# Stick-breaking attention: two subtractions per score tile written for VectorE instead of GpSimd

## The chip, the cores and the metric

The kernel runs on one core of a Trainium2 chip. Its time is the device time of one execution in microseconds (us). The core has five engines that work side by side and wait for each other through semaphores: TensorE (PE in the rows; its weight loads are PEld), VectorE (DVE), ScalarE (ACT), GpSimd (POOL) and SyncE (SP), which issues DMAs here. Each engine works through its own instructions in a fixed order.

## The reference

The reference is a block of two mixers, a memory attention and a mixture of experts on 1024 rows of width 1024, all in float32. Only one part of the first mixer matters here, the stick-breaking attention, 4 heads of width 64:

```python
for i in range(t // SB_BLOCK):                      # 8 blocks of 128 queries
    n_keys = (i + 1) * SB_BLOCK
    z = einsum('bhtd,bhsd->bhts', q_blk, k_blk) * scale
    strict = s_pos < t_pos
    log_beta = log_sigmoid(z)
    log_1m_beta = where(strict, log_sigmoid(-z), 0.0)
    between = cumsum(log_1m_beta, axis=3, reverse=True) - log_1m_beta
    weights = where(strict, exp(log_beta + between), 0.0)
    outs.append(einsum('bhts,bhsv->bhtv', weights, v_blk))
```

The weight of a key is the exponential of its logit less the sum of log(1 + exp(z)) over that key and all later ones. The kernel makes log(1 + exp(z)) as log(1 + exp(min(z, 40))) plus the part of z that lies over 40.

## The kernel before

The first mixer runs twice, once for each half of the rows (`first_mixer(h, ...)`, h = 0 and 1). In each half it makes projections (`proj_fm`, `proj_tm`), whose weights come in slabs: ScalarE rounds a slab to `whi`, VectorE subtracts to get `wlo`, and TensorE multiplies three times (`mm3`, lines 140 to 142, tile `mm`). Two further mixers of gated linear attention (`gla_pair`, tiles `qp`, `kp`, `d`, `E`, `cmp`, `at`) run in the same stretch.

The stick-breaking attention goes over 4 query blocks per half, 2 pairs of heads, chunks of at most 512 keys and the 2 heads of a pair. One pass through the innermost loop is called a unit here: 16 units in the first half, 32 in the second; 24 of the 48 are 512 keys wide, and 8 each are 128, 256 and 384 wide. A unit is a chain over four engines:

1. TensorE makes the logits (line 761), ScalarE copies them to `z`, and on the block's diagonal GpSimd masks 128 columns (line 768).
2. VectorE writes `e` = min(z, 40) (tile `ze`), GpSimd writes `cu` = z - e.
3. ScalarE overwrites `e` with exp(e) and then with ln(1 + e).
4. VectorE's running sum (line 775) adds `e` and `cu` from the last key to the first; where more chunks follow, its end is copied to `cy`.
5. GpSimd writes z = z - cu, ScalarE takes exp(z) in place.
6. TensorE transposes the result (tile `tp`), VectorE copies it to `pt` (line 787), TensorE multiplies with the values (tile `os`, line 790).

The tiles `z`, `ze`, `zc` (for `cu`) and `zp` (for `pt`) have two buffers each, so two units are under way at a time. Their instructions, the projections and the gated attention are merged into one order per engine by a scheduler when the program is built; units come first in it where they are ready, and the projections' matmuls fill what is left of TensorE. The scheduler has its own idea of how long an instruction takes. The helpers `TT` (line 41, two tensors) and `TS` (line 45 with one operation, line 47 with two) record most of VectorE's and GpSimd's instructions, so a line alone does not say which instruction it is; the tile names do.

Of the kernel before, what the change touches and what calls it, by code (L numbers as in the profile page):

```python
# [27 lines left out]
def block_kernel(  # L28
# [6 lines left out]
    pe, act, dve, pool, sp = nc.tensor, nc.scalar, nc.vector, nc.gpsimd, nc.sync  # L35

    def A(o, i, f, **kw):
        act.activation(out=o, in_=i, func=f, **kw)  # L38

    def TT(o, a, b, op, eng=None):  # L40
        (eng or dve).tensor_tensor(out=o, in0=a, in1=b, op=op)  # L41

    def TS(o, a, s1, op0, s2=None, op1=None, eng=None):
        if op1 is None:
            (eng or dve).tensor_scalar(out=o, in0=a, scalar1=s1, scalar2=None, op0=op0)
        else:
            (eng or dve).tensor_scalar(out=o, in0=a, scalar1=s1, scalar2=s2, op0=op0, op1=op1)

    def STT(o, a, s, b, op0, op1, **kw):
        dve.scalar_tensor_tensor(out=o, in0=a, scalar=s, in1=b, op0=op0, op1=op1, **kw)  # L50

    MUL, ADD, SUB, MAX, MIN, POW = (
        ALU.mult, ALU.add, ALU.subtract, ALU.max, ALU.min, ALU.pow)
# [10 lines left out]
    def bank(tag, bufs):  # L64
        return ps[0].tile([128, 512], F32, name=tag, tag=tag, bufs=bufs)
# [4 lines left out]
    def tpb():  # L70
        return bank("tp", 2)
# [121 lines left out]
    def transpose4(o, srcs):  # L193

        for j, s in enumerate(srcs):
            pe.transpose(o[0:s.shape[-1], j * 128:j * 128 + s.shape[0]], s, ident[0:s.shape[0], 0:s.shape[0]])  # L196
# [232 lines left out]
    with ad_stack:  # L429
# [15 lines left out]
        for k in range(8):  # L445
            gk = 8 // G
            j = k % gk
            if j == 0:
# [12 lines left out]
                for i in range(8):  # L461
                    w = was[k // gk * 8 + i][:, 1]
# [12 lines left out]
               eng=pool if k < 6 else dve)  # L475
# [217 lines left out]
    def first_mixer(h, hT, ahead):  # L693
# [36 lines left out]
        for pr in range(2):  # L730
            g = tpb()
            pe.matmul(out=g, lhsT=w2[:, 128 * pr:128 * pr + 128], rhs=lrs, start=True, stop=True)
            e = a1.tile([128, HALF], F32, name="spe", tag="E", bufs=3)
# [13 lines left out]
        for t in range(4):  # L747

            with tc.high_priority(offset=0):
                n = 4 * h + t  # L750
                os_ = bank("os", 1)
                carry0 = [True]
                for pr in range(2):
                    carry = [None, None]
                    for s0 in range((n // 4) * 4, -1, -4):
                        ns = min(4, n + 1 - s0)
                        w = ns * 128
                        for hh in range(2):
                            r = slice(64 * hh, 64 * hh + 64)
                            zp = bank("z", 1)  # L760
                            pe.matmul(out=zp[:, 0:w], lhsT=qc[r, pr, t * 128:(t + 1) * 128],
                                      rhs=kc_full[r, pr, s0 * 128:s0 * 128 + w], start=True, stop=True)
                            z = a1.tile([128, HALF], F32, name="z", tag="z", bufs=2)
                            e = a1.tile([128, HALF], F32, name="ze", tag="ze", bufs=2)
                            A(z[:, 0:w], zp[:, 0:w], AF.Copy)
                            if s0 + ns - 1 == n:
                                dg = slice(w - 128, w)
                                pool.affine_select(out=z[:, dg], in_=z[:, dg], pattern=[[-1, 128]], compare_op=ALU.is_gt,
                                                   fill=-30000.0, base=0, channel_multiplier=1)
                            TS(e[:, 0:w], z[:, 0:w], 40.0, MIN)  # L770
                            cu = a1.tile([128, HALF], F32, name="cu", tag="zc", bufs=2)
                            TT(cu[:, 0:w], z[:, 0:w], e[:, 0:w], SUB, eng=pool)
                            A(e[:, 0:w], e[:, 0:w], AF.Exp)
                            A(e[:, 0:w], e[:, 0:w], AF.Ln, bias=1.0)
                            dve.tensor_tensor_scan(out=cu[:, 0:w][:, ::-1], data0=cu[:, 0:w][:, ::-1],
                                                   data1=e[:, 0:w][:, ::-1],
                                                   initial=0.0 if carry[hh] is None else carry[hh], op0=ADD, op1=ADD)
                            if s0:
                                cy = a1.tile([128, 1], F32, name="cy", tag="cy", bufs=3)
                                dve.tensor_copy(out=cy, in_=cu[:, 0:1])  # L780
                                carry[hh] = cy
                            TT(z[:, 0:w], z[:, 0:w], cu[:, 0:w], SUB, eng=pool)
                            A(z[:, 0:w], z[:, 0:w], AF.Exp)
                            tp = tpb()
                            transpose4(tp, [z[:, j * 128:(j + 1) * 128] for j in range(ns)])
                            pt = a1.tile([128, HALF], F32, name="pt", tag="zp", bufs=2)
                            dve.tensor_copy(out=pt[:, 0:w], in_=tp[:, 0:w])
                            hd = pr * 2 + hh
                            for j in range(ns):
                                pe.matmul(out=os_[:, hd * 64:hd * 64 + 64], lhsT=pt[:, j * 128:(j + 1) * 128],  # L790
                                          rhs=vc_full[:, s0 + j, hd * 64:hd * 64 + 64],
                                          start=(hd == 0 and carry0[0]), stop=(hd == 3 and s0 == 0 and j == ns - 1))
                                carry0[0] = False
                A(y_sb[:, t], os_[:, 0:256], AF.Copy)
# [81 lines left out]
    def second_rows():  # L876
# [4 lines left out]
        return xt  # L881

    yT = first_mixer(0, hT0, early(second_rows, scale=scc, bias=shc))
    with tc.issue_after(ada_last[-1]):
        sp.dma_start(out=fnw, in_=final_norm_w.partition_broadcast(128))
    ada_gate()
    resid_out(0, yT, w_out[0], 8, x[0], u_d, 0, mul=gate_d)
    hT = late()
    yT = first_mixer(1, hT, early(lambda: mix2_rows(0), scale=nmx))
    resid_out(1, yT, w_out[0], 8, x[0], u_d, 0, mul=gate_d)  # L890
    hT = late()
# [871 lines left out]
    with tc.manual_schedule():  # L1763
# [7 lines left out]
        for i, (nm, e, half) in enumerate(units):  # L1771
            if i + AHEAD < len(units) - 1:
                split_unit(i + AHEAD)
            w = parts.pop(i)
# [171 lines left out]
```

## Time and profile before

| | |
|---|---|
| median of 3 runs | 2107.94 us (2098.9 to 2108.58) |
| profiled execution | 2095.23 us, its span 2093.5 us |
| busy in the span | PE 1980.0 us (95%), DVE 1457.7 (70%), ACT 1194.7 (57%), POOL 693.0 (33%) |
| first half's units | 66 to 181 us |
| second half's units | 430 to 693 us |

The span is the time from the first to the last instruction that was profiled; the profiled execution's own time is 1.7 us more. TensorE's busy time counts the whole way of a matmul through the array, and matmuls overlap, so 95% does not mean that TensorE could do no more. GpSimd's durations are rough. The granted clock is 1.00 where TensorE runs at 2.4 GHz and 0.50 where it runs at 1.2 GHz.

### The profile page before, as it was taken

The numbers are of one execution on the slowest core, as the hardware profiler recorded it, in microseconds if no ns is written. First come the engines' busy times: TensorE is split into PE (matmuls) and PEld (weight loads), VectorE is DVE, ScalarE is ACT, GpSimd is POOL, SyncE is SP. The second block draws the span as 40 slices with busy tenths as digits, with TensorE's granted clock in tenths as the row PEclk, the third lists the DMA queues.
The fourth block names the chain that finished last, engine by engine and source line by source line (L and its number), as shares of the span: only waits on it lengthen the run. The fifth ranks groups of instructions, "written<-read, shape, count | busy, mean of one in ns | idle before, by whom it ended". The sixth has DMA issues, their size and how long they took to land. (4 is left out here: it accounts for less than half of the span.)

```text
span 2093.5 us, 33387 instructions
## 1 busy us (share of the span) xinstructions
PE 1980.0 (95%) x13066; PEld 1666.5 (80%) x13066; DVE 1457.7 (70%) x1988; ACT 1194.7 (57%) x1896; POOL 693.0 (33%) x563
## 2 busy tenths in 40 slices
PE   6999899999999999999999998997899999999997
PEld 3877796887777897889888897796688888888874
DVE  6476784556687754687556865764788888888885
ACT  5454553454465442466435543562777877787774
POOL 3352110144454100242002410013355555555545
PEclk9999999999998899999999999997899999999998
DMA  8212334621111154221632137454799999999986
GB/s 304 81 42 71 102 103 132 196 80 41 31 42 40 52 144 138 61 61 61 180 83 61 51 125 251 142 185 173 266 375 388 385 378 374 377 375 382 372 343 247
DMA packets 197849, 381.88 MB, mean 182 GB/s; under 512 B 30740, under 2 KB 155956, under 8 KB 171064
## 3 DMA queue, kind: packets, MB, share of 16 engines
q1 hardware_dynamic: 174376, 343.94, 46.7%
q10 hardware_dynamic: 14096, 18.98, 2.5%
q0 software_dynamic: 9216, 16.80, 2.2%
q8 instruction: 104, 1.70, 0.3%
q14 instruction: 57, 0.47, 0.1%
HBM read 356.58 MB, written 39.85 MB: 189 GB/s over the span
## 5 line engine op out<-in xcount | busy, mean ns | idle before, releaser
L41 DVE TENSOR_TENSOR elo<-eraw,ehi 128x2048 fp32r<-128x2048 f32 x192 | 427.0, 2248 | 76.1 <-ACT ehi L38 71.7
L38 ACT ACTIVATE ehi<-eraw 128x2048 fp32r<-128x2048 f32 x192 | 367.0, 1912 | 15.9 <-PE yo L142 13.8
L140 PE MATMUL mm<-whi,fs 128*128 128x256 f32 x1152 | 334.5, 292 | 2.1 <-ACT q L38 1.2
L141 PE MATMUL mm<-wlo,fs 128*128 128x256 f32 x1152 | 335.1, 292 | 0.8 <-DVE wlo L41 0.8
L142 PE MATMUL mm<-whi,fs 128*128 128x256 f32 x1152 | 332.7, 290 | 0.0
L41 DVE TENSOR_TENSOR wlo<-raw,whi 128x1024 fp32r<-128x1024 f32 x156 | 198.4, 1272 | 141.9 <-ACT whi L38 139.8
L38 ACT ACTIVATE whi<-raw 128x1024 fp32r<-128x1024 f32 x156 | 164.7, 1056 | 222.6 <-PE mm L142 89.3
L41 POOL TENSOR_TENSOR elo<-eraw,ehi 128x1024 fp32r<-128x1024 f32 x65 | 191.9, 2954 | 204.8 <-ACT ehi L38 204.7
L140 PEld LDWEIGHTS mm<-whi,fs 128*128 128x128 f32 x1152 | 224.9, 196 | 11.1 <-issue 6.0
L141 PEld LDWEIGHTS mm<-wlo,fs 128*128 128x128 f32 x1152 | 226.1, 196 | 9.3 <-issue 6.5
L142 PEld LDWEIGHTS mm<-whi,fs 128*128 128x128 f32 x1152 | 224.7, 196 | 6.1 <-issue 5.9
L140 PE MATMUL gu<-ehi,xh 128*128 128x512 f32 x512 | 207.6, 406 | 0.0
L141 PE MATMUL gu<-elo,xh 128*128 128x512 f32 x512 | 202.3, 395 | 0.5 <-DVE elo L41 0.4
L142 PE MATMUL gu<-ehi,xl 128*128 128x512 f32 x512 | 202.3, 395 | 0.0
L140 PE MATMUL mm<-fs,whi 128*128 128x512 f32 x480 | 192.9, 405 | 5.1 <-DVE cq L50 2.0
L141 PE MATMUL mm<-fs,whi 128*128 128x512 f32 x480 | 193.5, 403 | 1.6 <-DVE fs L50 1.6
L142 PE MATMUL mm<-fs,wlo 128*128 128x512 f32 x480 | 192.8, 402 | 0.0
L140 PEld LDWEIGHTS mm<-fs,whi 128*128 128x128 f32 x480 | 92.1, 192 | 31.8 <-issue 5.3
L142 PEld LDWEIGHTS gu<-ehi,xl 128*128 128x128 f32 x512 | 96.7, 189 | 22.3 <-DVE xl L41 0.2
L141 PEld LDWEIGHTS gu<-elo,xh 128*128 128x128 f32 x512 | 97.0, 189 | 20.9 <-DVE elo L41 1.4
L140 PEld LDWEIGHTS gu<-ehi,xh 128*128 128x128 f32 x512 | 96.9, 189 | 19.6 <-ACT xh L38 0.2
L142 PEld LDWEIGHTS mm<-fs,wlo 128*128 128x128 f32 x480 | 92.2, 192 | 23.3 <-issue 4.6
(512 smaller groups left out, 4313.8 us busy)
## 6 DMA issues: line engine op xcount, KB each, us to landing
eraw<-in_w_e_gate_dram SPq DMA_DIRECT2D x64, 1024.0 KB, 9.6
eraw<-in_w_e_up_dram SPq DMA_DIRECT2D x64, 1024.0 KB, 8.2
eraw<-in_w_e_down_dram SPq DMA_DIRECT2D x64, 1024.0 KB, 8.1
raw<-in_w_in_dram SPq DMA_DIRECT2D x92, 512.0 KB, 3.7
raw<-in_w_out_dram SPq DMA_DIRECT2D x32, 512.0 KB, 3.6
wa<-in_w_ada_dram SPq DMA_DIRECT2D x8, 1024.0 KB, 10.5
fy<-y_d SPq DMA_DIRECT2D x6, 1024.0 KB, 6.8
xp<-in_x_dram SPq DMA_DIRECT2D x16, 256.0 KB, 4.4
```

Of the source, the lines that this page charges most:

```text
L38: act.activation(out=o, in_=i, func=f, **kw)
L41: (eng or dve).tensor_tensor(out=o, in0=a, in1=b, op=op)
L140: pe.matmul(out=o, lhsT=l[0], rhs=r[0], start=start, stop=False)
L141: pe.matmul(out=o, lhsT=l[0], rhs=r[1], start=False, stop=False)
L142: pe.matmul(out=o, lhsT=l[1], rhs=r[0], start=False, stop=stop)
```

## The change

In each unit the two subtractions that GpSimd made are made by VectorE. The first is written in another way: the part of z over 40 is max(z - 40, 0), one instruction with one tensor and two constants, which no longer reads `e`. The second stays a subtraction of two tensors. GpSimd keeps the mask of line 768.

```diff
                             TS(e[:, 0:w], z[:, 0:w], 40.0, MIN)
                             cu = a1.tile([128, HALF], F32, name="cu", tag="zc", bufs=2)
-                            TT(cu[:, 0:w], z[:, 0:w], e[:, 0:w], SUB, eng=pool)
+                            TS(cu[:, 0:w], z[:, 0:w], -40.0, ADD, 0.0, MAX)
                             A(e[:, 0:w], e[:, 0:w], AF.Exp)
...
-                            TT(z[:, 0:w], z[:, 0:w], cu[:, 0:w], SUB, eng=pool)
+                            TT(z[:, 0:w], z[:, 0:w], cu[:, 0:w], SUB)
                             A(z[:, 0:w], z[:, 0:w], AF.Exp)
```

The scheduler builds another order from it, on all engines, within the two stretches that hold the first mixer; before, between and behind them the orders are the same but for a few places. In three places:

VectorE at the seventh unit of the second half (fifth query block, third head, keys 0 to 511), before: `ze` is the minimum, `cu` the running sum (printed as SCALAR_TENSOR_TENSOR here), `cmp` belongs to the gated attention.

```order
L775 SCALAR_TENSOR_TENSOR cu<-cu,cy,ze 128x512
L566 COPY_PREDICATED cmp<-lmask,at_5590 128x32x8
L566 COPY_PREDICATED cmp<-lmask,at_5590 128x64x4
L787 COPY pt<-tp 128x128
L566 COPY_PREDICATED cmp<-lmask,at_5590 128x128x2
L564 COPY_PREDICATED cmp<-lmask,at_5590 128x256
```

The same unit on VectorE with the change, from its minimum to its second subtraction:

```order
L45 TENSOR_SCALAR ze<-z 128x512
L47 TENSOR_SCALAR cu<-z 128x512
L41 TENSOR_TENSOR wlo<-raw,whi 128x1024
L787 COPY pt<-tp 128x128
L775 SCALAR_TENSOR_TENSOR cu<-cu,cy,ze 128x512
L41 TENSOR_TENSOR qp<-q,E 128x256
L41 TENSOR_TENSOR kp<-k,E 128x512
L41 TENSOR_TENSOR z<-z,cu 128x512
```

The two new instructions (line 47 on `cu`, line 41 on `z`) stand in VectorE's order; the first directly behind the minimum, the second behind the running sum with a `qp` and a `kp` of the gated attention in between. In 23 of the 48 units something stands between the running sum and the second subtraction, in 25 nothing (or only the copy to `cy`).

TensorE in the first half, behind the logits of the sixth unit (first row), before:

```order
L761 MATMUL z<-kc_full,qc 128x256
L140 MATMUL mm<-whi,fs 128x256
L141 MATMUL mm<-wlo,fs 128x256
L142 MATMUL mm<-whi,fs 128x256
L547 MATMUL at_1283<-qp,kp 64x64 x8
L550 MATMUL at_1283<-qp,kp 64x32 x16
L196 MATMUL tp<-ident,z 128x128
```

and with the change, behind the same first row:

```order
L761 MATMUL z<-kc_full,qc 128x256
L142 MATMUL mm<-whi,fs 128x256
L547 MATMUL at_1283<-qp,kp 64x64 x8
L550 MATMUL at_1283<-qp,kp 64x32 x16
L761 MATMUL z<-kc_full,qc 128x256
L790 MATMUL os<-vc_full,pt 128x64
```

The transposition of an earlier unit (`tp`) has gone ahead of the first row, and the logits of the seventh unit, which came 26 rows behind the first row, come 4 rows behind it: the units follow each other with fewer matmuls of the projections in between.

GpSimd in the first half, a piece of the difference:

```order
-L768 AFFINE_SELECT z<-z 128x128
-L41 TENSOR_TENSOR cu<-z,ze 128x384
-L41 TENSOR_TENSOR z<-z,cu 128x384
-L768 AFFINE_SELECT z<-z 128x128
-L41 TENSOR_TENSOR cu<-z,ze 128x384
-L768 AFFINE_SELECT z<-z 128x128
-L41 TENSOR_TENSOR cu<-z,ze 128x384
-L41 TENSOR_TENSOR d<-P 128x512
-L41 TENSOR_TENSOR z<-z,cu 128x384
```

Only the masks and the subtractions `d` of the gated attention stay on GpSimd.

## Rows read from the trace of the kernel before

**Rows 1.** Busy time of each engine by stretch (us, count in brackets), with granted clock.

```profile
core 0: us, PE busy (x) PEld busy (x) DVE busy (x) ACT busy (x) POOL busy (x), PEclk, DMA share, GB/s
60.00:200.00 140.00, 134.92 (x1215) 113.61 (x1214) 87.92 (x133) 70.64 (x148) 58.54 (x62) 0.98 0.20 57
430.00:700.00 270.00, 256.50 (x2204) 210.42 (x2203) 190.01 (x290) 147.17 (x287) 114.18 (x105) 0.93 0.16 46
...
630.00:700.00 70.00, 68.70 (x662) 58.51 (x661) 55.97 (x89) 39.85 (x76) 28.75 (x22) 0.85 0.14 39
```

**Rows 2.** TensorE's waits, 60 to 790 us: total us, times, longest.

```profile
PE tp L196 <- ACT z L38: 8.2, 6, 2.4
...
PE os L790 <- DVE pt L787: 5.3, 4, 2.3
...
PE at L550 <- DVE kp L41: 2.8, 3, 1.4
...
PE os L790 <- DVE cy L780: 1.4, 1, 1.4
```

**Rows 3.** Timeline of one unit: start, duration, what, [idle before it <-releaser].

```profile
478.04 0.43 DVE L45 TENSOR_SCALAR ze<-z 128x512 f32<-128x512 f32 x1
...
478.55 1.27 POOL L41 TENSOR_TENSOR cu<-z,ze 128x512 f32<-128x512 f32 x1 [1.37 <-DVE ze L45]
...
479.85 1.29 ACT L38 ACTIVATE ze<-ze 128x512 f32<-128x512 f32 x2 [1.35 <-POOL cu L41]
...
481.25 1.28 DVE L775 TENSOR_TENSOR_SCAN cu<-cu,cy,ze 128x512 f32<-128x512 f32 x1 [2.78 <-ACT ze L38]
...
482.68 1.27 POOL L41 TENSOR_TENSOR z<-z,cu 128x512 f32<-128x512 f32 x1 [2.86 <-DVE cu L775]
...
483.98 1.11 ACT L38 ACTIVATE z<-z 128x512 f32<-128x512 f32 x2 [2.84 <-POOL z L41]
...
484.67 0.90 PE L196 MATMUL tp<-ident,z 128*128 128x128 f32 x3 [2.36 <-ACT z L38]
```

**Rows 4.** ScalarE's waits in 60 to 700 us, the longest in total.

```profile
ACT ze L38 <- POOL cu L41: 49.5, 34, 3.6
```

**Rows 5.** GpSimd's groups, 60 to 700 us: busy us, mean ns | idle before.

```profile
L41 POOL TENSOR_TENSOR d<-P 128x512 f32<-128x512 f32 x56 | 74.4, 1342 | 100.9 <-DVE P L508 66.7 <-ACT E L38 33.3 <-PE at L597 0.5
L41 POOL TENSOR_TENSOR cu<-z,ze 128x512 f32<-128x512 f32 x24 | 35.0, 1458 | 35.8 <-DVE ze L45 35.1 <-DVE cy L780 0.7
L41 POOL TENSOR_TENSOR z<-z,cu 128x512 f32<-128x512 f32 x24 | 33.4, 1393 | 58.9 <-DVE cu L775 56.0 <-PE mm L141 2.9
```

**Rows 6.** Instructions on `cu` alone, both stretches summed (60:200, 430:700).

```profile
sum 410.00, DVE 49.74 POOL 108.54; mean DVE 24.87 POOL 54.27
```

**Rows 7.** VectorE's groups, 60 to 700 us, columns as in rows 5.

```profile
L41 DVE TENSOR_TENSOR wlo<-raw,whi 128x1024 fp32r<-128x1024 f32 x69 | 91.4, 1325 | 69.4 <-ACT whi L38 68.9 <-PE tp L196 0.2
L41 DVE TENSOR_TENSOR kp<-k,E 128x512 f32<-128x512 f32 x39 | 37.8, 968 | 0.0
L41 DVE TENSOR_TENSOR qp<-q,E 128x256 f32<-128x256 f32 x54 | 33.5, 625 | 4.4 <-PE at L547 2.3 <-PE at L550 1.5 <-ACT E L38 0.5
...
L45 DVE TENSOR_SCALAR ze<-z 128x512 f32<-128x512 f32 x24 | 15.3, 638 | 1.4 <-ACT z L38 1.0 <-POOL z L768 0.2
```

**Rows 8.** Two tiles' instructions, whole span: shortest/median/longest ns, and shapes.

```profile
L41 DVE TENSOR_TENSOR kp<-k,E x48: 398/684/1781, 99.5 to 700.4; 128x512 f32<-128x512 f32 x40, 128x256 f32<-128x256 f32 x8
...
L45 DVE TENSOR_SCALAR ze<-z x48: 208/402/1532, 68.6 to 680.4; 128x512 f32<-128x512 f32 x24, 128x128 f32<-128x128 f32 x8, 128x256 f32<-128x256 f32 x8, 128x384 f32<-128x384 f32 x8
```

**Rows 9.** Timeline around 607 us, VectorE and GpSimd at the same time.

```profile
604.51 2.96 POOL L41 TENSOR_TENSOR d<-P 128x512 f32<-128x512 f32 x2 [2.62 <-DVE P L508]
...
606.50 2.05 DVE L41 TENSOR_TENSOR wlo<-raw,whi 128x1024 fp32r<-128x1024 f32 x1 [0.31 <-ACT whi L38]
...
607.43 2.25 POOL L41 TENSOR_TENSOR z<-z,cu 128x512 f32<-128x512 f32 x1
```

**Rows 10.** Two stretches of 5 us with a low granted clock, columns as in rows 1.

```profile
485.00:490.00 5.00, 5.00 (x22) 4.34 (x21) 2.10 (x3) 1.74 (x4) 1.51 (x2) 0.50 0.00 0
...
670.00:675.00 5.00, 5.00 (x21) 4.39 (x20) 3.88 (x4) 1.89 (x7) 4.70 (x4) 0.50 0.00 0
```

## The prediction

> **What bounds the kernel now.** I began with the busy time by stretch, because the change touches only the stretches in which the stick-breaking units run [rows 1]. In both, TensorE is busy for 95 to 96% of the time, VectorE for 63 and 70%, GpSimd for about 42%. TensorE is the bound, so GpSimd's work costs nothing by itself. It can cost only where TensorE waits for a unit, or where a wait is followed by a lower clock. TensorE's waits come next [rows 2]. Six times a transposition waits for a unit's last exponential (8.2 us in all), four times the product with the values waits for the copy `pt` (5.3 us), once for the copy `cy` (1.4 us). That is 14.9 us of direct waits in 2095. The third place to look is the granted clock [rows 1]: 0.98 over 140 us and 0.93 over 270 us. If TensorE's work scales with it, 0.02 x 140 + 0.07 x 270 = 21.7 us are lost in these stretches. Part of that follows a wait: the clock is 0.50 in the 5 us right behind the 2.36 us wait for a unit [rows 3, 10]. Part does not: in 670 to 675 us it is also 0.50 though TensorE never idles there [rows 10]. So direct waits and clock together are 36.6 us, and this is about the most that a perfect unit chain could return.
>
> **The change part by part: what it removes.** GpSimd loses 96 instructions, 108.5 us [rows 6]; a 512-wide pair costs 1.46 + 1.39 us [rows 5]. The subtractions `d` stay, 74.4 us [rows 5].
>
> The chain of a unit gets shorter in two places, as one undisturbed unit shows [rows 3]. The minimum ends at 478.47, GpSimd subtracts until 479.82, and only then does ScalarE start on `e`, since it overwrites what GpSimd reads. All units together make ScalarE wait 49.5 us so [rows 4]. After the change, `cu` no longer reads `e`: exp can start some 0.1 us behind the minimum, as GpSimd's start did, and the new instruction on `cu` (0.43 us, as the minimum) lies beside exp and ln (1.29 us). That takes 1.3 us out. The running sum ends at 482.53, GpSimd's second subtraction at 483.95; with VectorE's 0.68 us [rows 8] and 0.1 us of passing on, it would be 483.3: another 0.65 us. Together 1.95 us of the 2.36 us for which TensorE waits there. At GpSimd's mean durations it is 1.4 + 0.8 = 2.2 us.
>
> This is not all kept. At this very unit the order puts a `qp` and a `kp` between the running sum and the new subtraction, 0.40 + 0.68 us clean [rows 8], so the saving is about 0.9 us there. In 23 of 48 units something stands in that place; priced by the same rows it is some 21 us over 48 units, 0.45 us for a mean unit. I take 1.5 us as the mean shortening.
>
> **What it adds.** VectorE gets 48 subtractions and 48 two-constant instructions. The trace has no such instruction from z to cu, so I bound it. Clean: two-tensor instructions take 0.68 us at 512 and 0.40 at 256 [rows 8], by the line through these 0.54 at 384 and 0.26 at 128; 24 x 0.68 + 8 x (0.54 + 0.40 + 0.26) = 26 us. The one-tensor instructions, as the minimum, take 0.43 at 512 [rows 3] and 0.21 at 128 [rows 8], in between 0.36 and 0.28: 10.3 + 6.8 = 17 us. Low end 43 us. High end, at the means that VectorE shows beside GpSimd (0.968 for 0.684, and 0.638 for 0.43 [rows 3, 7, 8]): 26 x 1.42 + 17 x 1.48 = 62 us. I take the low end plus a little, 45 us, since most of the GpSimd work that stretches them goes.
>
> **What it gives back on VectorE.** One instruction on `wlo` takes 2.05 us, against a mean of 1.33, while GpSimd ends a `d`; and GpSimd's next subtraction takes 2.25 us against a mean of 1.39 [rows 5, 7, 9]. So the two engines hold each other up. The surplus that I can price is kp 39 x (0.968 - 0.684) = 11 us, qp 54 x (0.625 - 0.40) = 12 us, the minimum 24 x (0.638 - 0.43) = 5 us [rows 7, 8]: 28 us. Of GpSimd's work on tensors, 108.5 of 183 us goes, so 0.6 x 28 = 17 us come back; the bounds are 0 (all of the surplus is from `d`) and 28. Net VectorE goes from 278 us [rows 1] to about 306 of 410 us, 75%. This is hidden behind TensorE as long as `wlo`, `kp` and `pt` are still made in time. I charge 2 us for more queueing, with 0 and 15 as ends.
>
> The Trainium skill (SBUF — State Buffer, section on the two separate sides) says that VectorE and GpSimd share a port pair as an exclusive lock, and that a two-input VectorE instruction and a GpSimd instruction block each other outright. The stretched pair [rows 9] agrees: 2.05 and 2.25 us, each longer by about the rest of what the other had begun. Taken strictly, all surplus next to these 96 instructions goes; this is the third rival below.
>
> **What moves.** The scheduler uses the shorter chain at once: in the order shown, the logits of the seventh unit move up from 26 rows behind the sixth to 4. Fewer projections' matmuls then cover each chain. So I don't count 1.5 us for each wait, but only that what GpSimd's stretched durations added beyond a plan goes away.
>
> **The sum.** Direct waits: of 14.9 us I take 8 off, the transpositions' 6 waits with up to 1.5 us each being the main part; ends 0 and 14.9. Clock: of 21.7 us, 8 us off, those that follow such waits; ends 0 and 16. VectorE's queue: + 2 us. Total - 14 us. The profiled execution's 2095.23 us gives 2081. That execution is below all of the three timed runs; the mean of the four is 2102.7, and the median of a new set will lie nearer to it, so I forecast 2102.7 - 14 = 2089 us.
>
> **The rivals.**
> *The new order spends the gain.* The units are packed closer, so TensorE reaches the transpositions earlier by as much as the chain is shorter, and the 14.9 us of waits stay as they are, at other places. For it: the order's excerpt on TensorE; against it: 34 of ScalarE's starts on `e` were late by GpSimd [rows 4], most of them without TensorE's noticing. Time: 2103, from 2096 to 2108.
> *VectorE becomes the bound in the last stretch.* In 630 to 700 us it is busy for 56.0 of 70 us [rows 1]. About ten 512-wide units run there, each with 1.11 us more: 67 of 70 us if nothing comes back. From 95% on, every `pt` and `wlo` waits its turn; TensorE then waits for `pt` as in the four cases of before [rows 2], some 1.3 us each, for twelve units more: + 16 us, 2118. Against it: `d` and the moved subtractions stretch VectorE exactly here, GpSimd being busy for 28.75 of the 70 us, so part comes back. It decides if less than about 5 us do.
> *The relief is whole.* If the two engines truly lock each other out, the full 28 us come back, VectorE's `kp` and `cmp` are in time, and the waits for `pt` go too: direct waits - 13, clock - 14, + 2: - 25 us, 2078.
>
> **How the numbers follow.** The forecast (2089, its own range 2083 to 2095) has 0.42, the spent gain 0.25, VectorE as the bound 0.19, the whole relief 0.14. A change below 0.5% (10.5 us) can't be told from none here; the three runs alone spread by 9.7 us. About three quarters of the first case lie beyond that, with the whole relief 0.46 for faster; the rest of it, all of the spent gain and a little of the others make 0.36 for the same; slower 0.18. The range reaches from 2066, below the whole relief, to 2112, part of the way to VectorE as the bound, which leaves out about 2 in 10.
>
> **What would show it.** Right: GpSimd's busy time falls by some 108 us, no wait of ScalarE's `ze` for GpSimd is left, exp starts within 0.2 us of the minimum, the means of `kp` and `qp` fall towards 0.7 and 0.45 us, TensorE's waits for `z` and `pt` fall below 8 us, and the clock in 430 to 700 us rises above 0.95. Wrong: VectorE is over 90% busy in 630 to 700 us and TensorE's waits for `pt`, `kp` or `wlo` grow; or the waits for `z` stay at 8 us with the units closer together; or the clock falls just as often, because it follows the small matmuls of the gated attention and not the waits.

## The result and the profile after

| | before | changed |
|---|---|---|
| median | 2105.61 us (2098.9 to 2108.58) | 2077.76 us (2068.47 to 2082.54) |
| ratio | 1 | 0.9876 [0.9839, 0.9913] |
| profiled execution, span | 2095.23, 2093.5 us | 2068.47, 2066.8 us |

The changed kernel is faster by 1.2%. A second set of runs on another occasion (below, "changed again") gave 0.9911 [0.9885, 0.9937], 2081.72 against 2101.93 us: so 20 to 28 us. The forecast was 14 us less and 2089 us.

Where the time went. The next stage (its first matmul is at line 1148) starts at 822.0 us before and at 795.3 us now, 26.7 us earlier, and the end of the span also comes 26.7 us earlier. Nothing is won or lost behind the first mixer. The second half's first logits come 6.8 us earlier (419.4 against 426.2 us), so some 20 of the 26.7 us are won behind them. The busy time by stretch (columns as in rows 1) of the changed kernel, first the two stretches with units, then the last 70 us with units (their last logits are done at 630.4 us now, at 677.3 before), then all from 60 us to the next stage:

```profile
60.00:200.00 140.00, 138.94 (x1249) 116.69 (x1248) 92.30 (x170) 73.46 (x153) 28.46 (x34) 1.00 0.22 65
430.00:700.00 270.00, 260.66 (x2390) 217.15 (x2389) 208.48 (x371) 153.09 (x291) 37.43 (x41) 0.96 0.17 48
575.00:645.00 70.00, 67.70 (x584) 55.33 (x583) 60.47 (x96) 47.09 (x88) 13.07 (x11) 0.98 0.19 54
60.00:795.00 735.00, 709.11 (x6021) 602.90 (x6020) 497.31 (x838) 370.65 (x721) 103.14 (x113) 0.97 0.31 91
```

The same view of the kernel before, from 60 us to its next stage:

```profile
60.00:822.00 762.00, 723.14 (x6022) 613.43 (x6020) 488.67 (x742) 369.65 (x722) 208.71 (x209) 0.95 0.30 88
```

These two long rows hold the same work (6022 and 6021 matmul groups, 742 VectorE instructions and 742 + 96), so their differences are the whole effect. TensorE's idle time is the length less its busy time: 38.9 us before, 25.9 us now, 13.0 less. The clock's own records give 71.7 us at 0.50 before and 44.4 us now; half of that is lost to the low clock, 35.8 and 22.2 us, 13.6 less. Together 26.6 of the 26.7 us. This account holds in all 14 profiles of this study: the next stage starts at 746 us plus TensorE's idle time plus half of its time at 0.50, within 2.1 us.

TensorE's waits of the changed kernel between 60 and 790 us answer to [rows 2] (total us, times, longest):

```profile
PE mm L140 <- DVE mst L41: 4.2, 2, 2.4
PE os L790 <- DVE pt L787: 3.2, 4, 1.3
...
PE tp L196 <- ACT z L38: 2.6, 4, 1.0
...
PE at L550 <- DVE kp L41: 0.8, 2, 0.6
```

The waits for a unit (`z`, `pt`, `cy`) fall from 14.9 to 5.8 us. TensorE's waits for the gated attention's `kp` and `cmp` fall too. One of them is in rows 2; these two of the kernel before, same view, are not:

```profile
PE at L573 <- DVE cmp L564: 2.0, 3, 1.1
...
PE at L550 <- DVE cmp L566: 1.3, 2, 1.0
```

VectorE's groups by form, 60 to 700 us (columns as in rows 5), answer to [rows 7]:

```profile
L41 DVE TENSOR_TENSOR qp<-q,E 128x256 f32<-128x256 f32 x56 | 29.2, 528 | 3.9 <-PE at L547 2.1 <-PE at L550 1.7
L41 DVE TENSOR_TENSOR kp<-k,E 128x512 f32<-128x512 f32 x40 | 29.1, 727 | 0.0
...
L41 DVE TENSOR_TENSOR z<-z,cu 128x512 f32<-128x512 f32 x24 | 18.7, 780 | 0.3
...
L45 DVE TENSOR_SCALAR ze<-z 128x512 f32<-128x512 f32 x24 | 11.6, 482 | 7.3 <-ACT z L38 4.8 <-POOL z L768 2.3
L47 DVE TENSOR_SCALAR cu<-z 128x512 f32<-128x512 f32 x24 | 10.9, 456 | 0.0
```

The new subtraction takes 0.78 us on average at 512, the new instruction on `cu` 0.46. `kp` falls from 968 to 727 ns, `qp` from 625 to 528, the minimum from 638 to 482. The timeline of the unit that the order's excerpt showed, the seventh of the second half, which rows 3 show before:

```profile
466.11 0.42 DVE L45 TENSOR_SCALAR ze<-z 128x512 f32<-128x512 f32 x1
...
466.44 0.42 DVE L47 TENSOR_SCALAR cu<-z 128x512 f32<-128x512 f32 x1
...
466.67 1.28 ACT L38 ACTIVATE ze<-ze 128x512 f32<-128x512 f32 x2
...
469.02 0.29 DVE L787 COPY pt<-tp 128x128 f32<-128x128 f32 x1 [1.00 <-PE tp L196]
469.23 1.27 DVE L775 TENSOR_TENSOR_SCAN cu<-cu,cy,ze 128x512 f32<-128x512 f32 x1
...
471.34 0.69 DVE L41 TENSOR_TENSOR z<-z,cu 128x512 f32<-128x512 f32 x1
...
472.06 1.12 ACT L38 ACTIVATE z<-z 128x512 f32<-128x512 f32 x2 [1.25 <-DVE z L41]
```

The exponential starts 0.14 us behind the minimum. But the running sum stands behind a copy `pt`, which waits for TensorE, and the subtraction behind `qp` and `kp`: from the minimum's start to the last exponential's it is 5.95 us, and before it was 5.94 [rows 3]. This unit's chain is not shorter at all, and TensorE does not wait for it, where it waited 2.36 us before.

### The profile page after: what moved, and what is told of

Read it like the earlier page. It is cut to its first block, busy times and chain, and to the rows that moved or that the text cites. A ratio compares the mean times of both kernels' runs of the same rounds, so it can differ in the third digit from the quotient of the medians.

```text
span 2066.8 us, 33406 instructions
## 1 busy us (share of the span) xinstructions
PE 1966.1 (95%) x13066; PEld 1656.4 (80%) x13066; DVE 1466.3 (71%) x2084; ACT 1196.0 (58%) x1896; POOL 590.6 (29%) x467
## 5 line engine op out<-in xcount | busy, mean ns | idle before, releaser
L41 POOL TENSOR_TENSOR d<-P 128x512 f32<-128x512 f32 x56 | 74.4, 1346 | 218.9 <-ACT E L38 108.8
L140 PEld LDWEIGHTS mm<-fs,whi 128*128 128x128 f32 x480 | 91.5, 191 | 34.1 <-issue 5.8
L142 PEld LDWEIGHTS gu<-ehi,xl 128*128 128x128 f32 x512 | 96.4, 188 | 22.2 <-DVE xl L41 0.2
L140 PEld LDWEIGHTS gu<-ehi,xh 128*128 128x128 f32 x512 | 96.8, 189 | 19.5 <-ACT xh L38 0.2
```

Of the source, the lines that this page charges most:

```text
L140: pe.matmul(out=o, lhsT=l[0], rhs=r[0], start=start, stop=False)
L142: pe.matmul(out=o, lhsT=l[1], rhs=r[0], start=False, stop=stop)
```

## The experiments

Two theories stood after the result. **A, the chain:** a unit's chain is shorter by the hop (the stop at GpSimd between two steps on other engines), so TensorE waits less and its clock falls less. **B, the hold-up:** GpSimd's two-tensor work and VectorE's hold each other up, and taking the one away makes everything on VectorE punctual. Each median is of 4 to 12 executions. The table gathers what the text below reads; VectorE, GpSimd and TensorE's idle time are from one profile each, 60 us to the next stage; the chain is worked out from the trace, from the start of the minimum to the start of the last exponential, mean of the 48 units. A profiled execution need not be a typical one: that of "changed" is 9.3 us below its median, that of "idle VectorE work" 7.9 below, those of "second edit alone" and "add-max on GpSimd" 6.5 and 6.4 above.

| kernel | median us | ratio to before | VectorE us (count) | GpSimd us | TensorE idle us | half of time at 0.50 | chain us |
|---|---|---|---|---|---|---|---|
| before | 2101.80 to 2105.61 | 1 | 488.7 (742) | 208.7 | 38.9 | 35.8 | 6.59 |
| changed | 2077.76 | 0.9876 [0.9839, 0.9913] | 497.3 (838) | 103.1 | 25.9 | 22.2 | 4.42 |
| changed again | 2081.72 | 0.9911 [0.9885, 0.9937] | 498.6 (838) | 103.7 | 28.8 | 29.0 | 4.44 |
| first edit alone | 2086.48 | 0.9924 [0.9902, 0.9946] | 487.1 (790) | 153.0 | 31.0 | 34.1 | 4.95 |
| second edit alone | 2104.22 | 1.0007 [0.9987, 1.0026] | 502.0 (790) | 154.8 | 39.0 | 52.9 | 6.24 |
| add-max on GpSimd | 2090.89 | 0.9940 [0.9917, 0.9963] | 493.9 (790) | 180.6 | 31.4 | 42.7 | 4.64 |
| two tensors on VectorE | 2082.26 | 0.9906 [0.9884, 0.9928] | 513.7 (838) | 101.2 | 30.1 | 32.4 | 5.15 |
| idle GpSimd work | 2110.29 | 1.0036 [1.0014, 1.0058] | 546.1 (838) | 218.0 | 42.6 | 52.9 | 5.02 |
| idle VectorE work | 2089.77 | 0.9949 [0.9931, 0.9967] | 533.8 (934) | 101.4 | 37.3 | 23.9 | 5.03 |
| gated subtractions too | 2082.19 | 0.9911 [0.9882, 0.9940] | 505.5 (894) | 32.5 | 31.4 | 37.5 | 4.53 |
| idle GpSimd writes | 2086.93 | 0.9930 [0.9912, 0.9948] | 505.8 (838) | 203.3 | 27.4 | 37.5 | 4.58 |
| idle GpSimd work later | 2124.20 | 1.0107 [1.0088, 1.0126] | 539.3 (838) | 217.3 | 51.8 | 52.9 | 5.01 |
| maximum first | 2085.20 | 0.9922 [0.9906, 0.9939] | 498.2 (838) | 102.7 | 30.4 | 37.5 | 4.65 |
| hop through GpSimd | 2083.68 | 0.9916 [0.9895, 0.9938] | 504.5 (838) | 175.8 | 30.7 | 29.0 | 7.20 |

All edits below are against the changed kernel. The scheduler builds another order for each, which none of these experiments holds fixed.

**Each edit alone.** The first edit alone (the second subtraction back on GpSimd):

```diff
-                            TT(z[:, 0:w], z[:, 0:w], cu[:, 0:w], SUB)
+                            TT(z[:, 0:w], z[:, 0:w], cu[:, 0:w], SUB, eng=pool)
```

> Only the part over 40 moves to VectorE as an add and a maximum; the logit less the sums stays a subtraction on GpSimd. It removes about 56 us of GpSimd work and the wait of exp for GpSimd. Theory A (the shorter chain makes TensorE's waits and the clock dips after them go away; 1.3 of the 1.95 us that the chain loses are in this edit): about two thirds of the 26 us, some 2088 us beside 2104 of before and 2078 of both edits. Theory B (the gain is that VectorE and GpSimd no longer hold each other up, by GpSimd's time that goes): half, 2091 us, and the means of kp and qp fall half of the way. The waits of ScalarE's ze for GpSimd are zero under both.

The second edit alone (the part over 40 again by GpSimd from two tensors):

```diff
-                            TS(cu[:, 0:w], z[:, 0:w], -40.0, ADD, 0.0, MAX)
+                            TT(cu[:, 0:w], z[:, 0:w], e[:, 0:w], SUB, eng=pool)
```

> Only the second subtraction moves to VectorE; the part over 40 stays a subtraction of two tensors on GpSimd, which exp waits for. It removes about 52 us of GpSimd work and 0.65 us of the chain. Theory A: a third of the gain or less, 2096 us. Theory B: half, 2091 us. ScalarE's ze still waits some 50 us for GpSimd.

The first brings 0.9924, the second nothing that can be told from zero, 1.0007. In the second, ScalarE still waits for GpSimd and TensorE still waits for `z` as long as before; its waits, ScalarE's over 60 to 700 us and TensorE's over 60 to 790 us:

```profile
ACT ze L38 <- POOL cu L41: 47.0, 32, 3.3
...
PE tp L196 <- ACT z L38: 8.0, 9, 2.0
```

This alone would speak for A, since only the first edit takes a hop out that GpSimd's wait shows. But the two edits differ in more than the hop, so the next runs separate what the first one changes.

**Is it the engine, or the way the first instruction is written?** The add and maximum on GpSimd, which exp no longer waits for:

```diff
-                            TS(cu[:, 0:w], z[:, 0:w], -40.0, ADD, 0.0, MAX)
+                            TS(cu[:, 0:w], z[:, 0:w], -40.0, ADD, 0.0, MAX, eng=pool)
```

> As the changed kernel, but the add and maximum is made by GpSimd. It reads only z, so exp still need not wait, and GpSimd's time for it lies beside exp and ln. Theory A: nearly the whole gain stays, 2080 us, less a little where GpSimd is not done when ln is. Theory B: GpSimd works 50 us or more beside VectorE again, so about half the gain is gone, 2091 us, and kp and qp take longer than in the changed kernel.

And the old subtraction of two tensors on VectorE, which exp does wait for:

```diff
-                            TS(cu[:, 0:w], z[:, 0:w], -40.0, ADD, 0.0, MAX)
+                            TT(cu[:, 0:w], z[:, 0:w], e[:, 0:w], SUB)
```

> As the changed kernel, but the part over 40 is made by VectorE as z less its minimum, two tensors, so that exp has to wait for it. No GpSimd work comes back; the chain is longer by about 0.7 us and VectorE has some 12 us more. Theory A: a part of the gain goes, about 2086 us. Theory B: the time stays within 3 us of the changed kernel, 2078 to 2081 us.

On GpSimd it keeps at least a part of the gain, 0.9940, though the instruction takes 2.1 us there, as GpSimd's group (60 to 700 us) shows:

```profile
L47 POOL TENSOR_SCALAR cu<-z 128x512 f32<-128x512 f32 x24 | 50.8, 2117 | 76.1 <-ACT z L38 46.6 <-issue 19.9 <-DVE pt L787 6.1
```

With two tensors on VectorE the chain is 0.7 us longer than in the changed kernel and VectorE has 16 us more, and the gain is the same: 0.9906. So, on VectorE, the way of writing the first instruction is worth nothing by itself.

**The change again,** unaltered, beside the next three:

> The changed kernel unaltered, beside the three that follow, and once more against the kernel before. All theories: 0.987 to 0.989 of before, 2078 us.

It repeats the gain and shows how far one program's executions differ: idle time 25.9 and 28.8 us, but half of the low clock 22.2 and 29.0 us.

**Load without a chain.** Idle work for GpSimd behind the second subtraction, its result unread, about as much as the change took from GpSimd:

```diff
                             TT(z[:, 0:w], z[:, 0:w], cu[:, 0:w], SUB)
+                            TT(e[:, 0:w], e[:, 0:w], cu[:, 0:w], SUB, eng=pool)
+                            TT(e[:, 0:w], e[:, 0:w], cu[:, 0:w], SUB, eng=pool)
```

> The changed kernel with two more subtractions of a unit's width on GpSimd, of e less cu into e, behind the second subtraction; nobody reads their result, they only hold the two buffers of e and cu some 2.6 us longer. GpSimd has the 108 us of before again, two tensors each, while the units' chain stays short. Theory B (VectorE and GpSimd hold each other up): kp, qp and the minimum get as long as before (0.97, 0.63, 0.64 us) and at least half of the 26 us is lost, 2092 us or more. Theory A (the chain's length): within 5 us of the changed kernel.

Idle work for VectorE in the same place:

```diff
                             TT(z[:, 0:w], z[:, 0:w], cu[:, 0:w], SUB)
+                            TS(e[:, 0:w], e[:, 0:w], -40.0, ADD, 0.0, MAX)
+                            TT(e[:, 0:w], e[:, 0:w], cu[:, 0:w], SUB)
```

> The changed kernel with one more add-and-maximum and one more subtraction of a unit's width on VectorE, on e, behind the second subtraction; nobody reads their result. It gives VectorE the added 43 us of the change once more. If VectorE has room for it beside TensorE, as the prediction charged 2 us: within 4 us of the changed kernel. If VectorE is near to being the bound: 2090 us or more.

The idle work on GpSimd takes the whole gain away, 1.0036, though nobody waits for its result. The row by stretch of this kernel, columns as in rows 1:

```profile
60.00:841.00 781.00, 738.45 (x6024) 623.74 (x6024) 546.11 (x838) 371.31 (x722) 218.00 (x209) 0.93 0.29 86
```

VectorE runs the same 838 instructions as in the changed kernel and is busy for 546 us with them, not 497; summed one by one they take 48.8 us more. A piece of its timeline shows how:

```profile
574.22 3.15 POOL L41 TENSOR_TENSOR ze<-ze,cu 128x512 f32<-128x512 f32 x2 [3.30 <-DVE cu L775]
576.12 1.52 DVE L45 TENSOR_SCALAR ze<-z 128x512 f32<-128x512 f32 x1 [1.26 <-ACT z L38]
...
580.38 1.27 POOL L41 TENSOR_TENSOR ze<-ze,cu 128x512 f32<-128x512 f32 x1 [3.01 <-DVE cu L775]
580.79 1.40 DVE L41 TENSOR_TENSOR z<-z,cu 128x512 f32<-128x512 f32 x1
```

The minimum, 0.43 us clean, begins at 576.12 and ends at 577.64, just behind GpSimd's pair (577.37). The subtraction, 0.69 us clean, begins at 580.79 while GpSimd is at work until 581.65, and takes 1.40. VectorE's `kp` (60 to 700 us) is nearly as long as before [rows 7]:

```profile
L41 DVE TENSOR_TENSOR kp<-k,E 128x512 f32<-128x512 f32 x35 | 33.2, 949 | 0.0
```

TensorE's waits for `z` and `pt` are back, 60 to 790 us:

```profile
PE tp L196 <- ACT z L38: 14.0, 9, 4.1
PE os L792 <- DVE pt L789: 7.2, 7, 2.2
```

It is not that other work of GpSimd comes too late behind the idle work. VectorE's wait for the mask and ScalarE's for `d`, 60 to 700 us, are 8.0 and 8.7 us in the changed kernel and here

```profile
DVE ze L45 <- POOL z L768: 9.4, 15, 1.5
...
ACT E L38 <- POOL d L41: 5.7, 8, 1.3
```

The 21.2 us of TensorE's waits for `z` and `pt` above, 5.8 in the changed kernel, are the units' own: the hold-up reaches TensorE mostly through the units, though it does not make their chain as long as it was before.

On VectorE the idle work costs little: 44.6 us of added instructions, 8 us more time (2089.77 against 2081.72).

**The rest of the hold-up.** The gated attention's subtractions `d` on VectorE as well, in both places where they are made:

```diff
-                TT(dv_, Pv, Pv[:, :, B - 1:B].to_broadcast([128, nb, 2 * B]), SUB, eng=pool)
+                TT(dv_, Pv, Pv[:, :, B - 1:B].to_broadcast([128, nb, 2 * B]), SUB)
...
-        TT(d.rearrange("p (c t) -> p c t", t=128), P3, P3[:, :, 127:128].to_broadcast([128, 4, 128]), SUB, eng=pool)
+        TT(d.rearrange("p (c t) -> p c t", t=128), P3, P3[:, :, 127:128].to_broadcast([128, 4, 128]), SUB)
```

> The changed kernel with the subtractions d of the gated attention on VectorE too (64 of 128x512 in the first mixer, 0.68 us each, 44 us), so that GpSimd has nearly nothing left there. Theory B: the rest of the mutual hold-up goes (kp 0.68, qp 0.40 us) and pays for the added work, 2070 to 2078 us. Theory A: nothing in the units' chain changes but VectorE is fuller, 2078 to 2090 us.

VectorE's groups, 60 to 700 us:

```profile
L41 DVE TENSOR_TENSOR kp<-k,E 128x512 f32<-128x512 f32 x40 | 27.4, 684 | 0.0
...
L41 DVE TENSOR_TENSOR qp<-q,E 128x256 f32<-128x256 f32 x55 | 22.7, 418 | 5.2 <-PE at L547 4.2 <-PE at L550 0.7
```

Now `kp` and `qp` are at the clean price. The 56 moved subtractions take 38.3 us on VectorE and its other instructions 24.5 us less, but the time is the same, 0.9911. So moving them brings no time here, and no version here beats the changed kernel. What the relief would bring without the added work is not shown.

**Does it depend on reading, and on the place?** Idle writes on GpSimd, which read nothing:

```diff
                             TT(z[:, 0:w], z[:, 0:w], cu[:, 0:w], SUB)
+                            pool.memset(e[:, 0:w], 0.0)
+                            pool.memset(e[:, 0:w], 0.0)
+                            pool.memset(e[:, 0:w], 0.0)
+                            pool.memset(e[:, 0:w], 0.0)
+                            pool.memset(e[:, 0:w], 0.0)
```

> As the run with idle GpSimd work, but the two subtractions that nobody reads are replaced by five fills of e with zeros of a unit's width, about 0.52 us each at 512 and so 2.6 us a unit as before. GpSimd is as busy and holds e as long, but reads nothing. If GpSimd's queue, the held buffer or the order that the scheduler then builds took the gain away: 2105 to 2112 us again. If it was that VectorE's instructions on two tensors and GpSimd's hold each other up: kp, qp and the second subtraction fall back to 0.73, 0.53 and 0.78 us, and the time to 2085 us or less.

The idle two-tensor work behind the last exponential instead, out of the unit's own chain:

```diff
                             A(z[:, 0:w], z[:, 0:w], AF.Exp)
+                            TT(e[:, 0:w], e[:, 0:w], z[:, 0:w], SUB, eng=pool)
+                            TT(e[:, 0:w], e[:, 0:w], z[:, 0:w], SUB, eng=pool)
```

> As the run with idle GpSimd work, but its two subtractions read z after the last exponential, so that they can't begin at the very moment at which VectorE's second subtraction does. If only that collision in the chain counts (second subtraction 1.12 us there, 0.78 in the changed kernel): back to 2090 us or less. If any GpSimd work on two tensors beside VectorE counts: 2102 us or more.

The writes keep GpSimd busy for 203 us, nearly as long as the 218 of the idle reads, and most of the gain stays, 0.9930. VectorE's groups with the writes, 60 to 700 us:

```profile
L41 DVE TENSOR_TENSOR kp<-k,E 128x512 f32<-128x512 f32 x40 | 28.2, 706 | 0.0
...
L47 DVE TENSOR_SCALAR cu<-z 128x512 f32<-128x512 f32 x24 | 15.0, 623 | 0.0
L45 DVE TENSOR_SCALAR ze<-z 128x512 f32<-128x512 f32 x24 | 14.2, 591 | 6.8 <-ACT z L38 3.6 <-POOL z L768 2.3 <-POOL ze L786 0.7
```

`kp` is not stretched (706 ns, 727 in the changed kernel), the one-tensor instructions are (623 and 591, against 456 and 482). The later reads are worse than the kernel before, 1.0107. With them VectorE's groups read:

```profile
L41 DVE TENSOR_TENSOR qp<-q,E 128x256 f32<-128x256 f32 x49 | 37.5, 774 | 0.5 <-ACT E L38 0.4
L41 DVE TENSOR_TENSOR kp<-k,E 128x512 f32<-128x512 f32 x35 | 31.3, 894 | 0.0
```

It was not that the idle work kept buffers: waits for it are 0.7 us with the writes, 2.3 us with the later reads, and none with the first reads.

**The chain alone.** Two runs make the chain longer with little hold-up. The first has the add-max ahead of the minimum, so that exp waits for it (the table's chain starts at the minimum and leaves it out; from the start of the add-max it is 4.97 us):

```diff
-                            TS(e[:, 0:w], z[:, 0:w], 40.0, MIN)
...
                             TS(cu[:, 0:w], z[:, 0:w], -40.0, ADD, 0.0, MAX)
+                            TS(e[:, 0:w], z[:, 0:w], 40.0, MIN)
```

> The changed kernel with the add and maximum written ahead of the minimum. The same instructions and durations, exp starts some 0.45 us later, and the scheduler builds another order from it. It shows what another order of the same work is worth: within 5 us of the changed kernel if the order is of little weight, more if it is of much.

And the hop put back: three copies of 128 columns onto themselves on GpSimd, between the minimum and exp.

```diff
+                            pool.tensor_copy(out=e[:, 0:128], in_=e[:, 0:128])
+                            pool.tensor_copy(out=e[:, 0:128], in_=e[:, 0:128])
+                            pool.tensor_copy(out=e[:, 0:128], in_=e[:, 0:128])
                             A(e[:, 0:w], e[:, 0:w], AF.Exp)
```

> The changed kernel with three copies by GpSimd of 128 columns of e onto themselves between the minimum and exp. It puts a stop at GpSimd back into each unit's chain, some 1 to 1.5 us as the subtraction of before (1.46 us), behind whatever GpSimd has in its queue, but with one tensor read and only 128 columns, so that VectorE is held up little (kp about 0.75, second subtraction about 0.8 us). Theory A (the chain's length): most of the gain goes, 2095 us or more, and ScalarE's ze waits some 40 us for GpSimd. Theory B (the hold-up): 2088 us or less. In between: both count.

Both keep the gain, 0.9922 and 0.9916. With the hop, ScalarE waits for GpSimd again, and TensorE does not mind. ScalarE's wait (60 to 700 us) and TensorE's (60 to 790 us):

```profile
ACT ze L38 <- POOL ze L775: 28.2, 26, 2.3
...
PE tp L196 <- ACT z L38: 0.8, 3, 0.5
```

The chain is 7.20 us in the mean, longer than the 6.59 of the kernel before, and the time is that of the changed kernel. With the idle reads it is 5.02 and 5.01 us, shorter than before, and the gain is gone or more than gone. So A falls as the main cause: the time does not follow the mean length of the chain. The hop run carries this. From a unit's logits to its copy `pt` the idle reads take 16.1 and 16.3 us, which is more than the changed kernel's 13.6, and only the hop, with 17.0 (17.8 before), is as long and keeps the gain. The scheduler planned with the hop, so it is a longer chain in the plan that is shown to cost nothing.

## Why the prediction was right, and where its sizes were off

**The direction and the place** were right: faster, within the range, all of it within the first mixer, as less waiting and less low clock. GpSimd's busy time fell by 106 us (108 foretold), no `ze` waits for GpSimd, in the unit shown exp starts 0.14 us behind the minimum, `kp` is at 0.73 and `qp` at 0.53 us, TensorE's waits for `z` and `pt` are 5.8 us (below 8), the clock in 430 to 700 us is 0.96 (above 0.95). That the direction came out right is in part luck: the shorter chain and the smaller hold-up both pointed that way, and the working leaned on the one that the runs do not bear out.

**"Direct waits - 8":** the unit's waits fell by 9.1 us. What the step left out are TensorE's waits for `kp` and `cmp` of the gated attention: 6.1 us in the three rows of before, 0.8 in `kp`'s row of after and 0.4 for a `cmp`. Other waits grew (`mst`, from 1.8 to 4.2 us). All idle time together fell by 13.0 us in the first profile, by 10.1 in the second.

**"Clock - 8":** in the two stretches with units the granted clock gives 21.7 us lost before and 0.04 x 270 = 10.8 now, 11 us less. From 60 us to the next stage it is 13.6 us less in the first profile, 6.8 in the second. The step was right in kind, and its size is what differs from one execution to the next. The condition that the clock would fall just as often did come true: ten times from 60 us to the next stage, before and after. The stretches are shorter.

**"Given back 17", the step that failed in size.** Summed over all of VectorE's instructions up to the next stage, the new ones take 49.0 us (45 foretold; 18.7 + 10.9 us of it at 512, in the groups above), and those that were there before take 32.6 us less. That is twice the 17 that was taken, and above the bound of 28, which was priced on `kp`, `qp` and the minimum alone. `kp` at 512 gave back 9.4 us, `qp` 5.1 and the minimum at 512 3.7; the other 14 us came from groups that the sum took as undisturbed, `wlo` (3.3 us) first. All of VectorE's instructions together take 16 us more, but its busy time grew by 8.6 us only (it counts overlapping records once), so the "+ 2" for queueing had little to stand for. That real load on VectorE does cost a little is shown by the idle VectorE work.

**"What it removes", the chain, as the cause.** Its size was about right: the mean chain is 2.2 us shorter (1.5 foretold). Its role was not. The hop put back costs nothing, and the one unit on which the working rested is no shorter than before, yet TensorE does not wait for it. What the idle runs tie the gain to is the hold-up, which the prediction had as a smaller term and, taken whole, as its third rival ("the relief is whole", - 25 us). The result is nearest to that rival in size, though the relief is not whole: `d` remains, and `kp` is at 727 where 684 is clean.

The Trainium skill (SBUF — State Buffer, section Who interferes with whom) sharpens what the idle runs show: by it a VectorE instruction with two tensors in SBUF collides only with a GpSimd instruction that reads, and a one-tensor instruction in the two-port mode with any. The runs agree with both halves: `kp` 706 ns beside writes and 949 and 894 beside reads, the minimum 591 beside writes against 482. That the minimum runs in the two-port mode no run shows. The prediction's sentence from this page left out that the GpSimd instruction has to read.

**The other rivals.** The new order did not spend the gain. VectorE did not become the bound: in the last 70 us with units it is busy for 60.47 of 70 us, 86%, below the 95% from which that rival was to decide. Its price also had a wrong count: the trace of before has six 512-wide units whose minimum starts in 630 to 700 us, not about ten, so 6.7 us would have been added there, not 11.

**What stays open.** By the same sums the second edit alone gives VectorE back 13.2 us (for 29.6 us added) and brings no time; the first gives back 19.5 us (for 20.8) and brings 16 us of time. Together that is the 32.6 us of the whole change, so the relief adds up, but the time does not. In the second, GpSimd's own subtraction, which VectorE's work holds up, still stands ahead of exp. That would explain it, but the hop of copies stands there too and costs nothing. Nor is it shown why 45 us of added work on VectorE cost 8 us, and 49 and 41 us of hold-up cost 29 and 42: the scheduler may have planned for the one and not for the other, which no run shows, and each kernel also got an order of its own, and no run held the order fixed. Two things speak against the order as the cause. With the maximum first, the same work in another order, the time is 3.5 us from that of the changed kernel's second set (2085.20 and 2081.72). And how far an order departs does not sort the runs: of TensorE's 6020 matmul groups up to the next stage, the longest sequence in common with the changed kernel's is 5387 with the first idle reads, which lose the gain, and 5382 with the writes and 5361 with the hop, which keep it.

## What to carry to other kernels

Work that is put on GpSimd to relieve VectorE is not free there even when TensorE is the bound and nobody waits for its result: before leaving it there, compare the means of VectorE's instructions with their shortest ones, over all of VectorE's groups and not a few. If they stand apart as here (0.97 us for `kp` against 0.68), try the work on VectorE, for what moves may cost VectorE much less net: 49 us moved here, and its instructions took 16 us more in sum. And test a suspected chain by putting its length back without its load; here a longer chain cost nothing and a load that nobody waits for cost the whole gain.

## What the runs showed of the hardware

A GpSimd instruction with one tensor and two constants is slower than one with two tensors: 2.12 us against 1.46 at 512 columns. On VectorE the same add and maximum takes 0.46 us.

TensorE's clock also falls with no wait ahead of it. In the changed kernel's timeline, products with 64 columns follow each other without a gap from 653.5 us on, and the clock falls in their midst:

```profile
658.15 0.43 PE L621 MATMUL at<-Si,qs 64*128 64x64 f32 x2
658.51 0.55 PE L619 MATMUL at<-vv,stf 128*128 128x64 f32 x2
658.99 0.69 PE L621 MATMUL at<-Si,qs 64*128 64x64 f32 x2
...
665.14 0.41 PE L141 MATMUL mm<-wlo,fs 128*128 128x256 f32 x1
665.35 0.36 PE L142 MATMUL mm<-whi,fs 128*128 128x256 f32 x1
665.55 0.28 PE L140 MATMUL mm<-whi,fs 128*128 128x256 f32 x1
```

From 658.99 us a pair takes 0.69 us instead of 0.43. TensorE then waits 1.92 us for VectorE, up to 662.2, behind the fall, and only at 665.5 are the projections' matmuls back to 0.28. The records put the granted clock at 0.50 from 658.7 for 6.8 us. Two executions of one program differ in how much of this there is: 44 and 58 us at 0.50 up to the next stage, and 10 us in time.
